# High and low halves of the columns side by side in one matmul: a hybrid decoder trunk on one core

## The chip, the core and the metric

The kernel runs on one core of a Trainium2 chip. The metric is the device time of one execution in microseconds (us), the median of three runs. Inside one profiled execution the profile also gives the span of the core's own work, from its first instruction to its last.

## What is computed

The reference is a trunk of two pre-norm residual layers over 256 tokens of width 1024, in float32. Of each layer only the mixer matters here; after it comes a dense SwiGLU (layer 0) or a top-2-of-8 expert SwiGLU (layer 1).

```python
h = rms_norm(x, norm_mix[layer])
q, f_logit, i_in, g_out, b_gate, c_gate, u, gate_a, gate_b = split_projection(h, w_in)   # 1024 columns each
f = lb + (1 - lb) * sigmoid(f_logit);  k = (1 - lb) * sigmoid(-f_logit);  q = silu(q) * scale
o = rms_norm(recurrence(q, k, i_in, log(max(f, F_MIN)))) * silu(g_out)      # 8 heads of 128
conv = causal_depthwise_conv3(b_gate * u)
merged = sigmoid(gate_a) * (o @ w_proj_hgrn) + sigmoid(gate_b) * ((c_gate * conv) @ w_proj_conv)
x = x + merged @ w_out
```

## The kernel before

**Number format.** Every float32 product is done as three matmuls in a shorter format. A weight tile `w` is split into `wh` (its high part, made by ScalarE) and `wl` (the rest, made by VectorE); the activations are split into `hh` and `hl` likewise. The product is `wh*hh + wh*hl + wl*hh`, summed in PSUM.

**A stream and its loads.** `col(s, g)` names the g-th half (512 columns) of the s-th part of `w_in`: 0 queries, 1 forget gates, 2 and 3 value and output gate, 4, 6 and 5 the convolution's b, u and c, 7 and 8 the merge gates. `mm_cols` (L125 on) computes one such half with tokens in the free dimension: it loads the weights in two pieces of 1 MB with `wload` (4 rows of 128 by 512 columns each), and for each row block `kt` of 128 and each column block `ct` of 128 it issues three matmuls with 256 moving columns (the tokens): L139 `wh` by `hh`, L141 `wh` by `hl`, L143 `wl` by `hh`. A half is 32 such triples, 96 matmuls. Its four sums stand in one PSUM tile of 4 KB a partition, tag "mm", of which there are two.

**The weights' way.** `wload` (L77 to L94) issues the load on SyncE's queue into one of four buffers (more of them late in layer 1), then ScalarE copies the high part into one of three buffers (L91, `whi`), then VectorE subtracts for the low part into one of two buffers (L93, `wlo`). For the first four loads of a mixer these two steps are cut into pieces of 512 elements.

**What follows a stream.** In `mixer` (from L515 on) a finished PSUM tile is read by one VectorE instruction of 1024 elements a partition: `by_rbc` (L258), which multiplies by the per-token factor of the norm, or for u and c a product with what is there (L596, L614). Forget gates then go through two sigmoids and nine VectorE instructions, queries through a silu and a scaling.

**What runs beside.** `scores` (prefix products of the recurrence, mostly VectorE, with small matmuls) and `readout` are generators; each `tick()` after a weight piece adds one of their steps to the program. The three-tap convolution (L604 to L607, 24 VectorE instructions) reads `bu`, the product of b and u, and writes `cv`; the product of `cv` and c is split into `ych`, `ycl` (tags hlC and hlD) for the convolution's output projection, whose first weight piece meets the first half of `cv` and the second piece the second half.

**Order.** The source is not the order of the queues. The framework that compiles it places every instruction on its engine's in-order queue as soon as its inputs are expected to be there, and in source order among those that are ready; a tile with a tag is handed over when the last reader of the tile before it on that tag is done. The column tiles `hh` and `hl` are made by `cols` (L235) on tags hlA and hlB.

## Time and profile before

| | |
|---|---|
| median of 3 runs (lowest, highest) | 1512.69 us (1511.3, 1512.91) |
| the profiled execution, its own time | 1511.85 us |
| span of the core in it | 1510.1 us |
| mean granted clock of TensorE | 0.995 of full speed |
| TensorE matmul busy | 1462.3 us (97% of the span) |
| VectorE busy | 651.4 us (43%) |
| ScalarE busy | 394.4 us (26%) |
| read from HBM | 414.40 MB |

The span holds, in order, the mixer of layer 0 (to about 311 us), the dense SwiGLU (to about 500 us), the mixer of layer 1 (to about 801 us) and the experts (to the end). The mean shares of VectorE and ScalarE say little: nearly all their work lies in the first 800 us. The profile's engines are PE (TensorE matmul), PEld (TensorE weight load), DVE (VectorE), ACT (ScalarE), POOL (GpSimd) and SP (SyncE).

### The profile page before, as it was taken

To read this page: it belongs to the slowest core of one execution; us is meant where nothing else is said; L and a number is where in the kernel's file an instruction comes from. 1 tells how busy PE (TensorE), PEld (TensorE's weight loads), DVE (VectorE), ACT (ScalarE), POOL (GpSimd) and SP (SyncE) were. 2 spreads that over 40 slices of the span, in tenths; PEclk is the share of its full clock that TensorE was granted. 3 is DMA by queue.
4 is the path that set the end of the run, shared out by engine and by line. 5 is a ranking of instruction groups with operands and counts; after the bars stand their busy time and mean duration, and the time that the engine had idled before them with its cause. 6 is when DMAs were issued, how large, how long until landed. Compare 5 with 4: busy or idle time off the path is not lost.

```text
span 1510.1 us, 39658 instructions
## 1 busy us (share of the span) xinstructions
PE 1462.3 (97%) x18130; PEld 1203.4 (80%) x18130; DVE 651.4 (43%) x875; ACT 394.4 (26%) x484; POOL 41.7 (3%) x80
## 2 busy tenths in 40 slices
PE   7999999999999999999999999899999989999994
PEld 7989999999999998999996696557977554766751
DVE  6965776665455796568764202011121102011112
ACT  6544334454344554434442000000000000000000
POOL 3000011000000000001000000000000000000000
PEclk9999999999999999999999999999999999999998
DMA  8564544556556555555746899999999999999994
GB/s 270 181 194 157 169 140 170 194 168 195 186 178 197 166 194 170 168 168 203 285 168 226 290 402 409 410 413 406 411 373 402 408 413 409 408 412 359 411 410 184
DMA packets 135364, 418.15 MB, mean 277 GB/s; under 512 B 6784, under 2 KB 8928, under 8 KB 123920
## 3 DMA queue, kind: packets, MB, share of 16 engines
q1 hardware_dynamic: 134768, 414.26, 73.9%
q8 instruction: 146, 2.39, 0.7%
q0 software_dynamic: 384, 1.21, 0.3%
q14 instruction: 34, 0.28, 0.1%
q10 hardware_dynamic: 32, 0.01, 0.0%
HBM read 414.40 MB, written 1.05 MB: 275 GB/s over the span
## 4 chain that ended last, share of the span: by engine, by line
PE 89%; DMA 9%; DVE 1%; ACT 0%; issue 0%; SPq 0%; POOL 0%; POOLq 0%; DVEq 0%; ACTq 0%
PE psb L139 12%; PE pa L982 12%; PE psb L143 12%; PE psb L141 12%; PE pb L982 11%; PE ye L972 10%; DMA wraw<-in_expert_w_dram 8%; PE psa L160 3%; PE psa L162 3%; PE psa L161 3%; PE psc L1023 2%; PE y L708 1%; PE y L709 1%; PE y L710 1%; PE pg L920 1%; PE ye L964 1%
## 5 line engine op out<-in xcount | busy, mean ns | idle before, releaser
L139 PE MATMUL psb<-hlA,whi 128*128 128x256 f32 x1376 | 393.5, 286 | 3.2 <-ACT whi L91 3.2
L143 PE MATMUL psb<-hlA,wlo 128*128 128x256 f32 x1376 | 390.4, 284 | 0.8 <-DVE wlo L93 0.8
L141 PE MATMUL psb<-hlB,whi 128*128 128x256 f32 x1376 | 390.2, 284 | 0.0
L91 ACT ACTIVATE whi<-wraw 128x2048 fp32r<-128x2048 f32 (+1 forms) x165 | 251.7, 1543 | 376.6 <-PE psb L141 234.5
L93 DVE TENSOR_TENSOR wlo<-wraw,whi 128x2048 fp32r<-128x2048 f32 (+1 forms) x165 | 297.9, 1821 | 116.3 <-issue 40.4
L139 PEld LDWEIGHTS psb<-hlA,whi 128*128 128x128 f32 x1376 | 264.3, 192 | 4.6 <-ACT whi L91 3.6
L143 PEld LDWEIGHTS psb<-hlA,wlo 128*128 128x128 f32 x1376 | 264.2, 192 | 1.5 <-DVE wlo L93 1.3
L141 PEld LDWEIGHTS psb<-hlB,whi 128*128 128x128 f32 x1376 | 264.5, 192 | 0.5
L1055 DVE TENSOR_TENSOR sae<-sae,pb 128x768 f32<-128x768 f32 (+3 forms) x24 | 19.1, 796 | 454.5 <-PE pb L982 454.5
L972 PE MATMUL ye<-wraw,the 128*32 128x256 f32 x2640 | 150.5, 379 | 1.0 <-issue 1.0
L972 PEld LDWEIGHTS ye<-wraw,the 128*32 128x32 f32 x2640 | 104.8, 110 | 39.9 <-issue 2.5
L1054 ACT ACTIVATE sae<-pa 128x768 f32<-128x768 f32 (+3 forms) x24 | 16.4, 685 | 433.1 <-PE pa L982 433.1
L982 PE MATMUL pb<-wraw,bu 128*32 128x256 f32 (+1 forms) x2112 | 109.3, 362 | 2.4 <-DMA wraw<-in_expert_w_dram 1.8
L982 PE MATMUL pa<-wraw,bu 128*32 128x256 f32 (+1 forms) x2112 | 110.0, 362 | 0.7 <-DMA wraw<-in_expert_w_dram 0.7
L982 PE MATMUL pb<-wraw,hlD 128*32 128x256 f32 (+1 forms) x1920 | 100.8, 362 | 4.0 <-DMA wraw<-in_expert_w_dram 3.9
L982 PE MATMUL pa<-wraw,hlD 128*32 128x256 f32 (+1 forms) x1920 | 102.2, 362 | 0.7 <-DMA wraw<-in_expert_w_dram 0.7
L982 PEld LDWEIGHTS pb<-wraw,bu 128*32 128x32 f32 x2112 | 74.7, 110 | 34.3 <-issue 2.8
L982 PEld LDWEIGHTS pa<-wraw,bu 128*32 128x32 f32 x2112 | 73.2, 110 | 34.0 <-issue 4.9
L982 PEld LDWEIGHTS pb<-wraw,hlD 128*32 128x32 f32 x1920 | 71.3, 110 | 30.3 <-DMA wraw<-in_expert_w_dram 5.8
L982 PEld LDWEIGHTS pa<-wraw,hlD 128*32 128x32 f32 x1920 | 72.8, 110 | 26.3 <-issue 6.4
L964 PE MATMUL ye<-wraw,the 128*64 128x512 f32 x264 | 61.8, 601 | 10.7 <-DMA wraw<-in_expert_w_dram 10.7
L964 PEld LDWEIGHTS ye<-wraw,the 128*64 128x64 f32 x264 | 17.2, 136 | 51.2 <-issue 27.1
(259 smaller groups left out, 1459.3 us busy)
## 6 DMA issues: line engine op xcount, KB each, us to landing
wraw<-in_expert_w_dram SPq DMA_DIRECT2D x216, 1024.0 KB, 17.8
wraw<-in_w_in_dram SPq DMA_DIRECT2D x72, 1024.0 KB, 5.2
wraw<-in_expert_w_dram SPq DMA_DIRECT2D x64, 768.0 KB, 15.9
wraw<-in_dense_w_dram SPq DMA_DIRECT2D x33, 1024.0 KB, 5.1
wraw<-in_w_proj_conv_dram SPq DMA_DIRECT2D x8, 1024.0 KB, 5.1
wraw<-in_w_proj_hgrn_dram SPq DMA_DIRECT2D x8, 1024.0 KB, 5.1
wraw<-in_w_out_dram SPq DMA_DIRECT2D x8, 1024.0 KB, 5.2
xt<-in_x_dram SPq DMA_DIRECT2D x2, 512.0 KB, 3.8
```

The costliest lines, as they stand in the source:

```text
L91: nc.scalar.activation(hf[:, ks], rf[:, ks], AF.Copy)
L93: nc.vector.tensor_tensor(lf[:, ks], rf[:, ks], hf[:, ks].bitcast(F32), op=ALU.subtract)
L139: nc.tensor.matmul(o, wh[:, k, cs], hh[:, kt, :], start=first, stop=False, skip_group_check=True)
L141: nc.tensor.matmul(o, wh[:, k, cs], hl[:, kt, :], start=False, stop=False, skip_group_check=True)
L143: nc.tensor.matmul(o, wl[:, k, cs], hh[:, kt, :], start=False, stop=last, skip_group_check=True)
L160: nc.tensor.matmul(o, hh[:, kt, ts], wh[:, k, :], start=kt == 0, stop=False)
L161: nc.tensor.matmul(o, hh[:, kt, ts], wl[:, k, :], start=False, stop=False)
L162: nc.tensor.matmul(o, hl[:, kt, ts], wh[:, k, :], start=False, stop=kt == KT - 1)
L964: nc.tensor.matmul(out[64 * h:64 * h + 64, 0:n], stat, w[:, h * n:h * n + n], start=start, stop=stop, skip_group_check=True)
L972: nc.tensor.matmul(out(g)[32 * lane:32 * lane + 32, 0:n], by_lane(g if lane == 3 else lane, lane), w[:, c0:c0 + n], start=start and g != 1 ...
L982: nc.tensor.matmul(ps[32 * lane:32 * lane + 32, g, 0:n // 4], xf[:, kt, 32 * g:32 * g + 32], w[:, k, lane * n // 4:(lane + 1) * n // 4], s ...
L1023: nc.tensor.matmul(ps[:, o], PT[:, w, ts], y[:, part, c], start=i == part == 0, stop=part == 1 and i in (0, 3), skip_group_check=True)
```

## The change

The column tiles are laid out anew: tag hlA now holds row blocks 0 to 3 with high and low part side by side, 256 + 256 columns for each row block, and hlB row blocks 4 to 7. A small class `Part` gives the high or the low part as before, and `both(kt)` the 512 columns together.

A new function `mm_both` computes a half of 512 columns as two chunks of 256. A chunk has one weight load of 1 MB (8 row blocks by 256 columns) and its own PSUM tile: for each of its two column blocks one bank, whose first 256 columns take `wh*hh + wl*hh` and whose other 256 take `wh*hl`. For each `kt` and `ct` there are two matmuls: `wh` by both parts (512 moving columns) and `wl` by `hh` (256). At the end of a chunk ScalarE copies the second half of the banks to SBUF and VectorE adds the first half to it.

`mm_both` takes the place of `mm_cols` in nine halves of each layer: forget gates g = 1, both halves of the queries, and both halves of the convolution's b, u and c. The factor of the norm is then applied from SBUF. Two tiles are new: `uu` (tag hlC, which `ych` takes next) and `cc` (tag bu, after the convolution has read `bu`). All else is unchanged: forget gates g = 0, the merge gates, the dense layer and the output projections stay with `mm_cols`.

```diff
--- before.py
+++ after.py
@@ -147,6 +147,35 @@
             tick()
         return ps
 
+    class Part:
+
+        def __init__(self, tiles, part):
+            self.tiles, self.part = tiles, part
+
+        def __getitem__(self, at):
+            return self.tiles[at[1] // 4][at[0], at[1] % 4, self.part, at[2]]
+
+        def both(self, kt):
+            return self.tiles[kt // 4][:, kt % 4].rearrange("p i s -> p (i s)")
+
+
+
+    def mm_both(src2d, c0, hh, out):
+        for c in range(0, out.shape[1], 2):
+            ps = psum.tile([128, 2, 2, S], F32, tag="mm", name="psb")
+            wh, wl = wload(src2d, 0, KT, c0 + c * 128, 256)
+            for kt in range(KT):
+                for ct in range(2):
+                    cs = slice(ct * 128, ct * 128 + 128)
+                    nc.tensor.matmul(ps[:, ct].rearrange("p i s -> p (i s)"), wh[:, kt, cs], hh.both(kt), start=kt == 0,
+                                     stop=False, skip_group_check=True)
+                    nc.tensor.matmul(ps[:, ct, 0], wl[:, kt, cs], hh[:, kt, :], start=False, stop=kt == KT - 1,
+                                     skip_group_check=True)
+            tick()
+            o = out[:, c:c + 2, :]
+            nc.scalar.activation(o, ps[:, :, 1, :], AF.Copy)
+            nc.vector.tensor_tensor(o, o, ps[:, :, 0, :], op=ALU.add)
+
 
     def mm_toks(src2d, c0, hh, hl, after={}):
         ps = psum.tile([128, TT, 512], F32, tag="mm", name="psa")
@@ -234,7 +263,8 @@
 
     def cols(w, half):
         if half == 0:
-            cur["x"] = [big8(tag, [128, KT, S], F32R) for tag in ("hlA", "hlB")]
+            tiles = [big8(tag, [128, KT // 2, 2, S], F32R) for tag in ("hlA", "hlB")]
+            cur["x"] = [Part(tiles, i) for i in range(2)]
         hh, hl = cur["x"]
         for j in range(half * 2, half * 2 + 2):
             ps = transposed(xt, j)
@@ -532,9 +562,12 @@
         qall = big8("qq", [128, 2, 4, S])
         fc, kk, qq = ([a[:, g] for g in range(2)] for a in (fall, kall, qall))
         for g in range(2):
-            ps = mm_cols(wi, col(1, g), 512, hh, hl, enter if g == 0 else {})
             f, k = fc[g], kk[g]
-            by_rbc(f, ps)
+            if g == 0:
+                by_rbc(f, mm_cols(wi, col(1, g), 512, hh, hl, enter))
+            else:
+                mm_both(wi, col(1, g), hh, f)
+                by_rbc(f, f)
             nc.scalar.activation(k, f, AF.Sigmoid, scale=-1.0)
             nc.scalar.activation(f, f, AF.Sigmoid)
             for i in range(4):
@@ -544,8 +577,8 @@
                 nc.vector.tensor_scalar(k[:, i, :], k[:, i, :], om[:, l, hd:hd + 1], None, op0=ALU.mult)
             nc.vector.tensor_scalar(f, f, F_MIN, None, op0=ALU.max)
         for g in range(2):
-            ps = mm_cols(wi, col(0, g), 512, hh, hl)
-            by_rbc(qq[g], ps)
+            mm_both(wi, col(0, g), hh, qq[g])
+            by_rbc(qq[g], qq[g])
             nc.scalar.activation(qq[g], qq[g], AF.Silu)
             nc.vector.tensor_scalar(qq[g], qq[g], QSCALE, None, op0=ALU.mult)
 
@@ -588,12 +621,14 @@
 
         bu = big8("bu", [128, KT, S])
         for g in range(2):
-            ps = mm_cols(wi, col(4, g), 512, hh, hl)
-            by_rbc(bu[:, g * 4:g * 4 + 4, :], ps)
+            gs = slice(g * 4, g * 4 + 4)
+            mm_both(wi, col(4, g), hh, bu[:, gs, :])
+            by_rbc(bu[:, gs, :], bu[:, gs, :])
+        uu = big8("hlC", [128, KT, S])
         for g in range(2):
-            ps = mm_cols(wi, col(6, g), 512, hh, hl)
             gs = slice(g * 4, g * 4 + 4)
-            nc.vector.tensor_tensor(bu[:, gs, :], bu[:, gs, :], ps, op=ALU.mult)
+            mm_both(wi, col(6, g), hh, uu[:, gs, :])
+            nc.vector.tensor_tensor(bu[:, gs, :], bu[:, gs, :], uu[:, gs, :], op=ALU.mult)
             by_rbc(bu[:, gs, :], bu[:, gs, :])
         flush(1)
         if l % 2 == 1:
@@ -607,11 +642,12 @@
             nc.vector.scalar_tensor_tensor(cv[:, ct, 2:S], bu[:, ct, 0:S - 2], wc(0), cv[:, ct, 2:S],
                                            op0=ALU.mult, op1=ALU.add)
         ych, ycl = (big8(tag, [128, KT, S], F32R) for tag in ("hlC", "hlD"))
+        cc = big8("bu", [128, KT, S])
         for g in range(2):
-            ps = mm_cols(wi, col(5, g), 512, hh, hl)
             gs = slice(g * 4, g * 4 + 4)
             by_rbc(cv[:, gs, :], cv[:, gs, :])
-            nc.vector.tensor_tensor(cv[:, gs, :], cv[:, gs, :], ps, op=ALU.mult)
+            mm_both(wi, col(5, g), hh, cc[:, gs, :])
+            nc.vector.tensor_tensor(cv[:, gs, :], cv[:, gs, :], cc[:, gs, :], op=ALU.mult)
             split(cv[:, gs, :], ych[:, gs, :], ycl[:, gs, :])
         if l % 2 == 1:
             more("fc")
```

## Rows read from the trace of the kernel before

**Rows 1.** The page: busy time of each engine (first row), the DMA engines' mean busy tenths in 40 slices of the span (second row), and the chain of work that ended last, by engine and by line.

```profile
PE 1462.3 (97%) x18130; PEld 1203.4 (80%) x18130; DVE 651.4 (43%) x875; ACT 394.4 (26%) x484; POOL 41.7 (3%) x80
...
DMA  8564544556556555555746899999999999999994
...
PE 89%; DMA 9%; DVE 1%; ACT 0%; issue 0%; SPq 0%; POOL 0%; POOLq 0%; DVEq 0%; ACTq 0%
PE psb L139 12%; PE pa L982 12%; PE psb L143 12%; PE psb L141 12%; PE pb L982 11%; PE ye L972 10%; DMA wraw<-in_expert_w_dram 8%; PE psa L160 3%; PE psa L162 3%; PE psa L161 3%; PE psc L1023 2%; PE y L708 1%; PE y L709 1%; PE y L710 1%; PE pg L920 1%; PE ye L964 1%
```

**Rows 2.** Busy time by stretch. Columns: the stretch and its length in us, then for PE, PEld, DVE, ACT and POOL the busy us and in brackets the number of instructions, then the granted clock, the share of the DMA engines and GB/s. The stretches are those of layer 0: forget gates g = 1 and queries; the convolution's b; u; c.

```profile
27.00:61.40 34.40, 34.40 (x289) 34.40 (x288) 33.62 (x43) 19.37 (x13) 0.00 (x0) 1.00 0.53 176
...
159.50:186.00 26.50, 26.50 (x419) 25.80 (x405) 20.88 (x31) 9.82 (x10) 0.41 (x2) 1.00 0.50 169
186.00:214.00 28.00, 28.00 (x250) 27.46 (x248) 20.72 (x29) 10.73 (x20) 1.95 (x1) 1.00 0.39 126
214.00:240.80 26.80, 26.80 (x228) 26.80 (x228) 22.81 (x39) 11.33 (x29) 7.85 (x5) 1.00 0.44 145
```

**Rows 3.** Timeline of PE over the queries' first half (layer 0): start in us, length, engine, line, operation. Its first triple and its last matmul.

```profile
38.44 0.28 PE L139 MATMUL psb<-hlA,whi 128*128 128x256 f32 x1
38.56 0.28 PE L141 MATMUL psb<-hlB,whi 128*128 128x256 f32 x1
38.68 0.28 PE L143 MATMUL psb<-hlA,wlo 128*128 128x256 f32 x1
...
49.84 0.28 PE L143 MATMUL psb<-hlA,wlo 128*128 128x256 f32 x1
```

**Rows 4.** Timeline of PE in a value stream (512 moving columns): one triple, from one L160 to the next; the two matmuls between are left out.

```profile
70.38 0.39 PE L160 MATMUL psa<-whi,hlA 128*128 128x512 f32 x1
...
71.06 0.39 PE L160 MATMUL psa<-whi,hlA 128*128 128x512 f32 x1
```

**Rows 5.** Timeline of PE where 256 columns give way to 512 (288 us) and 512 to 256 (311 us).

```profile
288.45 0.28 PE L143 MATMUL psb<-hlA,wlo 128*128 128x256 f32 x1
288.57 0.40 PE L160 MATMUL psa<-whi,hlC 128*128 128x512 f32 x1
...
311.04 0.39 PE L162 MATMUL psa<-whi,hlD 128*128 128x512 f32 x1
311.26 0.28 PE L139 MATMUL psb<-hlA,whi 128*128 128x256 f32 x1
```

**Rows 6.** Groups of instructions by line with shapes kept apart: line, engine, operation, tiles, shapes, count | busy us, mean ns of one | idle time of the engine before them and its releasers. Two of DVE (an addition that reads PSUM; a product out of SBUF), then three of ACT and DVE (a copy out of PSUM; the two steps on the weights).

```profile
L644 DVE TENSOR_TENSOR xt<-xt,psa 128x512 f32<-128x512 f32 x8 | 5.2, 684 | 3.5 <-PE psa L673 2.3 <-PE psa L162 1.1
...
L258 DVE TENSOR_TENSOR bu<-bu,rbc 128x1024 f32<-128x1024 f32 x4 | 4.9, 1220 | 0.0
...
L413 ACT ACTIVATE st<-psx 128x512 f32<-128x512 f32 x4 | 2.3, 579 | 0.0
...
L91 ACT ACTIVATE whi<-wraw 128x2048 fp32r<-128x2048 f32 x117 | 224.3, 1917 | 357.4 <-PE psb L141 232.9 <-issue 91.5 <-PE psa L162 19.1
L93 DVE TENSOR_TENSOR wlo<-wraw,whi 128x2048 fp32r<-128x2048 f32 x117 | 267.5, 2286 | 107.0 <-issue 38.1 <-PE psa L161 22.9 <-PE psb L143 21.9
```

**Rows 7.** DMA over a stretch of the dense layer (446 to 460 us) in which weight pieces of 256 columns are loaded: packets by size, and the issues with size and median time to landing; the third row is the page's for the pieces of 512 columns.

```profile
DMA packets 2279, 2.52 MB, mean 180 GB/s; under 512 B 32, under 2 KB 2080, under 8 KB 2278
...
wraw<-in_dense_w_dram SPq DMA_DIRECT2D x3, 1024.0 KB, 5.4
...
wraw<-in_w_in_dram SPq DMA_DIRECT2D x72, 1024.0 KB, 5.2
```

**Rows 8.** Who waited for whom: the waiter, what it waited for: us in total, times, longest us.

```profile
ACT whi L91 <- PE psb L141: 234.5, 68, 4.7
```

**Rows 9.** Timeline of DVE beside the queries' first half: a reciprocal of the scores, the factor on forget gates g = 1, and the low part of the first weight piece of the queries' second half.

```profile
38.33 2.54 DVE L344 RECIPROCAL bu<-fc 128x384 f32<-128x384 f32 x1
40.79 1.15 DVE L258 TENSOR_TENSOR fc<-psb,rbc 128x1024 f32<-128x1024 f32 x1
...
47.01 2.27 DVE L93 TENSOR_TENSOR wlo<-wraw,whi 128x2048 fp32r<-128x2048 f32 x1
```

**Rows 10.** Timeline of DVE beside the convolution's c: the product of b and u (second half), the last instructions of the convolution, and the low part of the first weight piece of c, g = 1.

```profile
214.47 1.21 DVE L596 TENSOR_TENSOR bu<-bu,psb 128x1024 f32<-128x1024 f32 x1
...
223.67 0.87 DVE L607 SCALAR_TENSOR_TENSOR fc<-bu,pcol,fc 128x254 f32<-128x254 f32 x2
...
225.31 2.28 DVE L93 TENSOR_TENSOR wlo<-wraw,whi 128x2048 fp32r<-128x2048 f32 x1
```

**Rows 11.** Timeline of PE: last matmul of c, g = 0, first of c, g = 1, last of c, g = 1, first of the convolution's output projection.

```profile
227.34 0.28 PE L143 MATMUL psb<-hlA,wlo 128*128 128x256 f32 x1
...
229.17 0.36 PE L139 MATMUL psb<-hlA,whi 128*128 128x256 f32 x1
...
240.64 0.28 PE L143 MATMUL psb<-hlA,wlo 128*128 128x256 f32 x1
240.76 0.28 PE L139 MATMUL psb<-hlC,whi 128*128 128x256 f32 x1
```

**Rows 12.** Timeline of ACT and then of DVE after the end of c, g = 1: the next high part, the high part of the product, and its low part.

```profile
240.89 1.92 ACT L91 ACTIVATE whi<-wraw 128x2048 fp32r<-128x2048 f32 x1 [3.84 <-PE psb L141]
242.71 1.04 ACT L55 ACTIVATE hlC<-fc 128x1024 fp32r<-128x1024 f32 x1
...
244.30 1.22 DVE L56 TENSOR_TENSOR hlD<-fc,hlC 128x1024 fp32r<-128x1024 f32 x1
```

## The prediction

> **What bounds the kernel now.** I read the chain of waits first: PE holds 89% of it, the DMA engines 9%, VectorE 1% [rows 1]. The DMA share is the experts' weights: only in the last third of the slices are the DMA engines at 9 tenths and over [rows 1]. Then the busy times of the stretches that the change touches: PE is busy through all of them, at a granted clock of 1.00, the 2.4 GHz level; the DMA engines are at 0.39 to 0.53 [rows 2]. So in the mixer the end is set by the time between matmul starts. Beside it VectorE is the engine to watch: 33.6 of 34.4 us in the forget gates and queries, 21 to 23 of some 27 us in the convolution's streams [rows 2]. Third, the timelines of PE, DVE and ACT at the places where a stream ends, for how early each input of PE was ready. Whatever the two mixers gain or lose comes through to the end: the dense layer and the experts wait for them, and the expert weights' loads are released by the weight buffers that the mixer frees, which move with PE.
>
> **What the change takes away.** A half of 512 columns is 96 matmuls. From the first to the last of the queries' first half there are 95 steps in 49.84 - 38.44 = 11.40 us, so 120 ns from start to start with 256 moving columns [rows 3]. With 512 moving columns three steps take 71.06 - 70.38 = 0.68 us, 226.7 ns each [rows 4]. At 2.4 GHz the columns alone are 106.7 and 213.3 ns: both carry some 13.3 ns that do not grow with the columns. Two matmuls of 256 by the same weights are 240.0 ns, one of 512 is 226.7. A triple falls from 360.0 to 346.7 ns. The new order alternates the two sizes, and the trace has each passage once: 256 to 512 in 0.12 us, 512 to 256 in 0.22 us [rows 5], as if each ran among its like. I count nothing for it. 32 triples a half, nine halves a layer, two layers: 576 x 13.3 ns = **7.7 us less** on PE. The bounds of this term: the two passages of rows 5 add up to 0.34 us to the rounding of the rows, 0.35 at most, which would leave 10 ns a triple and 5.8 us; more than 7.7 no row shows.
>
> The Trainium skill (TensorE: Matmul & The Clock Gate, Back-to-back issue gap) puts the warm gap of a matmul by itself at its columns over 2.4 GHz plus 2.5 ns. By that a merged pair would save 2.5 ns and the change 1.4 us. The trace shows 13.3 ns in both sizes, so the measurement decides.
>
> **What it adds off PE.** Each of 36 chunks ends with a ScalarE copy of 512 elements out of PSUM, 0.58 us, and a VectorE addition that reads PSUM, 0.68 us [rows 6]: 21 us of ScalarE and 24.6 us of VectorE in all. The factor of the norm, 1.22 us, reads SBUF and not PSUM and costs the same [rows 6]. The weight loads stay as many and as large. Their rows shrink from 2 KB to 1 KB; the dense layer's last pieces have that shape already and land in 5.4 us against 5.2 [rows 7], four buffers ahead, with the DMA engines half idle. Nothing.
>
> The copy does not run at once. A new high part starts on ScalarE in the moment in which a chunk's matmuls free its buffer (68 such waits, 234.5 us [rows 8]). In a chunk the last matmul by `wh` stands one step ahead of the last by `wl`, so the 1.92 us high part [rows 6] is ready first and the copy stands behind it on the in-order queue. The sum of a chunk is then in SBUF some 1.92 + 0.58 + 0.68 + 0.2 (hand-overs, an estimate) = 3.4 us after its last matmul, 1.5 if the copy goes first. A chunk lasts 16 x 346.7 = 5.55 us, and PE needs that PSUM tile again one chunk later: 2.1 us to spare. So the shorter life of the PSUM tiles costs nothing where VectorE is free.
>
> **What is late next.** Three places have less room, each once a layer.
>
> *Queries.* The low part of the second half's first piece stands behind all the forget gates' work. It ends at 47.01 + 2.27 = 49.28 us, and PE needs it at 49.96 + 0.24 = 50.20 [rows 3, 9] (the half's last start plus one step, then two more): 0.9 us to spare. Two additions come ahead of it (0.68 each) and PE arrives 2 x 0.43 us sooner: 1.3 us short if all else keeps its place. But VectorE was full there with work that PE does not wait for yet, like the 2.54 us reciprocal at 38.33 us [rows 9]; some of it will move back. Between 0 and 1.3, I take 0.3.
>
> *The convolution's c.* `cc` takes over the buffer of `bu`, so no chunk of c leaves PSUM before the convolution has read its last `bu`: 223.67 + 0.87 = 224.5 us, and the low part after it ends at 227.6, while PE needs it at 229.17 + 0.24 = 229.4 [rows 10, 11]: 1.8 us to spare. From the end of u's first half to there VectorE gets four additions more (2.7 us) and PE comes 0.87 us sooner; that is 1.8 us short. Against it, the readout's products and a factor of the norm may move back, 2.3 us by their neighbours' rows. Between 0 and 3 (the sum and the delayed copy), I take 0.6.
>
> *The start of the output projection.* Its second piece, 48 steps of 120 ns after 240.76 us, at 246.5, needs the second half of the product of `cv` and c; that was ready at 244.30 + 1.22 = 245.5 [rows 11, 12], 1.0 us to spare. Before, the product (1.22 us) ran beside the high part of the weights (240.89 to 242.81 [rows 12]). Now it stands behind copy and addition, which stand behind that high part: 0.13 + 1.92 + 0.58 + 0.68 + 1.22 + 1.04 + 1.22 = 6.8 us after the last matmul's end, with hand-overs some 7, against 5.9 needed. 1.0 us short; 0 if the copy goes first. Between 0 and 2, I take 1.0.
>
> In b and u themselves VectorE keeps some 5 us of idle time in 26.5 [rows 2] against 2.7 us of additions in each stretch: nothing, at most 0.5.
>
> **The sum.** 7.7 less, 2 x (0.3 + 0.6 + 1.0) = 3.8 more: 3.9 us less. The profiled execution (1511.85 us, of which 1510.1 are the span) would come to 1508.0; the median of the runs stands 0.84 us above that execution, so **1508.8 us**.
>
> **The rivals.**
> - *The gain in full.* The copies go ahead of the high parts, and VectorE's deferrable work moves back at all three places. For it: that work is there [rows 9]. Against it: the high parts started at the first moment 68 times [rows 8]. 1512.7 - 7.7 = 1505.0 us.
> - *The gain is eaten.* All three places fall short by their full sums, 1.3 + 1.8 + 1.0 = 4.1 us a layer, 8.2 in all: 1513.2; with one of them half covered, 1511 to 1512. For it: VectorE at 98% in the queries [rows 2].
> - *Slower: c's sums wait for the convolution.* One mechanism: the handing over of `bu`'s buffer to `cc`. PE can do two chunks of c (11.1 us and the readout's matmuls between, some 2.7: 229.17 - 227.34 - 0.12 = 1.7 of them [rows 11], the rest within the half) before it needs the first PSUM tile back; from then on each us that the convolution ends later is a us of PE. If the product of b and u starts 3.4 us after u's last matmul, and two low parts (2.29 each) are placed ahead of the convolution's last instructions, its end is 3.4 + 4.6 = 8 us later than the 11.2 us after u's end of now (213.3 to 224.5), 19.2, and the copy and addition bring it to 20.5 against 13.8. 6.7 us a layer, 13.4 in all, less 7.7: 1518.4 us. It decides for slower from 3.9 us a layer on. Against it: the convolution stands ahead of those low parts in the source, and what is ready goes in source order.
> - *The merge saves nothing.* The 13.3 ns come back with the alternation of sizes, as a 360 ns triple: 0 less, 3.8 more, 1516.5 us. Rows 4 and 5 speak against it. The skill's 2.5 ns, if they held for this pair, would give 1512.7 - 1.4 + 3.8 = 1515.1 us.
>
> **How the numbers follow.** Forecast (1506.5 to 1509.7) 0.33; gain in full 0.20; eaten 0.28; merge saves nothing 0.06; slower 0.13. A measurement of this kernel tells about 0.2%, 3.0 us, from no change. Faster by more than that: forecast and full gain, 0.53. Within: the eaten gain, 0.28. Slower by more: the last two, 0.19. The range takes in the full gain and half a us below it, and above all of the eaten case with 2 us for the bounds of its terms: 1504.5 to 1515.5, with the last two rivals left out. The forecast's own range is 1506.5 to 1509.7.
>
> **What the profile after would show.** 512-column matmuls of `whi` by hlA or hlB, 576 of them, with starts 226.7 ns apart from the next, and triples of 347 ns; if the triple is 360 ns, the first term is wrong. ScalarE's copies 2 us after a chunk's last matmul, behind a high part; if they come at once, the third place has no wait. PE waiting for `wlo` in the queries, for the PSUM tile or `wlo` at c's g = 1, for hlD in the first projection: 0.3, 0.6 and 1.0 us, the same in both layers. A wait of PE for ScalarE or VectorE at every chunk, some us each, would mean that the sums come back later than one chunk, and would prove the whole account of the PSUM tiles wrong.

## The result, and the profile after

| | median of its runs | profiled execution | span | ratio to before |
|---|---|---|---|---|
| before | 1512.19 us (4 runs) | 1511.85 us | 1510.1 us | |
| after | 1522.54 us (4 runs) | 1522.33 us | 1520.6 us | 1.0056 [1.0038, 1.0073] |

The medians differ by 10.35 us. (The ratio is an estimate of its own with a 95% interval, not the quotient of these two medians.) The forecast was 1508.8 us, and the range ended at 1515.5. The question is where more than the gain went.

First, the merge. This is the timeline of PE early in forget gates g = 1, which begin at 30.02 us: the fourth pair of matmuls and the start of the fifth (start in us, length, engine, line, operation).

```profile
31.08 0.40 PE L170 MATMUL psb<-hlA,whi 128*128 128x512 f32 x1
31.31 0.28 PE L172 MATMUL psb<-hlA,wlo 128*128 128x256 f32 x1
31.43 0.40 PE L170 MATMUL psb<-hlA,whi 128*128 128x512 f32 x1
```

From start to start there are 0.23 and 0.12 us, so what was a triple takes 0.35 us; the forecast was 346.7 ns. The two sizes in alternation don't eat the gain, but it isn't whole everywhere: this half took 11.31 us, 353 ns a triple, and the queries' second half in layer 1 took 11.09 us, 346.6 ns.

Second, what PE waited for. Apart from the wait for the very first high part (4.1 us, before 3.2), three rows of its waits belong to the streams of the mixers and are new or longer (waiter, what it waited for: us in total, times, longest us; both layers together):

```profile
PE psb L172 <- DVE wlo L93: 4.2, 4, 1.7
...
PE psb L143 <- DVE wlo L93: 3.1, 3, 1.3
PE psb L139 <- ACT hlC L55: 0.4, 2, 0.2
```

The first two are waits for the weights' low part, which VectorE makes; before, those of L143 came to 0.8 us in all. The third is the convolution's projection, which waits for the high part of its input. None is for a PSUM tile.

Third, where. The start of every stream of weights can be read from the timeline of PE, and the difference of two starts is a stream's length. Sorted by parts, the span grew by 10.5 us so:

| part | change, us |
|---|---|
| up to the end of the first stream (forget gates g = 0, not merged) | +3.1 |
| forget gates g = 1 and queries, layers 0 and 1 | -0.5, -0.9 |
| b and u | -1.5, -1.5 |
| c and the first half of the convolution's projection | +5.5, +5.3 |
| the other streams of the mixers and the dense layer | -0.2 |
| experts and the stretch ahead of them | +1.1 |

So the merge gave 4.4 us in the streams ahead of c, and c with the projection's start took 10.8. The first and the last part hold no merged stream. At the start 1.0 us is the later begin of the first stream (13.28 against 12.30 us), and 2.1 us its pace. The windows after (the stretch and its length, busy us and instructions of PE, PEld, DVE, ACT and POOL, granted clock, DMA share, GB/s):

```profile
12.00:17.00 5.00, 3.72 (x15) 3.26 (x15) 3.66 (x9) 4.40 (x11) 1.74 (x4) 0.52 1.08 358
17.00:27.00 10.00, 9.54 (x60) 9.42 (x60) 7.54 (x19) 6.89 (x14) 0.53 (x1) 0.73 0.99 297
...
214.70:246.30 31.60, 29.21 (x178) 24.87 (x178) 27.45 (x42) 15.07 (x36) 5.88 (x5) 1.00 0.43 143
```

From 17 to 27 us the granted clock was 0.73 after and 1.00 before. The timeline of PE shows it too: the matmuls of the first stream start 0.21 us apart until 22.5 us, before until 16.9, and then 0.12. PE left the 1.2 GHz level 5.6 us later in this execution; ahead of that stream it had stood idle, 4.1 us of it for the first high part (3.2 before). The experiments show whether that is a price of the change. The third row is c's stretch: PE is busy 29.2 of 31.6 us at the full clock, where before it was busy all the time [rows 2]. It is c that has to be explained.

There, in layer 0, PE reads as follows (idle time before an instruction, and who ended it, in brackets):

```profile
230.36 0.50 PE L170 MATMUL psb<-hlA,whi 128*128 128x512 f32 x1
230.70 1.75 PE L253 MATMUL pst<-ident,tokA 128*128 128x128 f32 x9
232.38 0.50 PE L170 MATMUL psb<-hlA,whi 128*128 128x512 f32 x1
234.58 0.39 PE L172 MATMUL psb<-hlA,wlo 128*128 128x256 f32 x1 [1.70 <-DVE wlo L93]
...
240.02 0.71 PE L253 MATMUL pst<-ident,tokA 128*128 128x128 f32 x5
241.14 0.39 PE L172 MATMUL psb<-hlA,wlo 128*128 128x256 f32 x1 [0.42 <-DVE wlo L93]
...
254.97 0.39 PE L143 MATMUL psb<-hlC,wlo 128*128 128x256 f32 x1 [1.35 <-DVE wlo L93]
```

The first matmul by the low part of c, g = 1, comes 4.2 us after the first by the high part; before it was two steps, 0.24 us. The marked wait is only part of the loss: 14 of the readout's transposes (L253), which stood behind the projection's first half, now lie in this gap (9) and in the next (5). VectorE's timeline shows why the low part came late:

```profile
217.41 2.29 DVE L93 TENSOR_TENSOR wlo<-wraw,whi 128x2048 fp32r<-128x2048 f32 x1
...
219.69 0.68 DVE L177 TENSOR_TENSOR hlC<-hlC,psb 128x512 f32<-128x512 f32 x1
...
221.17 1.22 DVE L631 TENSOR_TENSOR bu<-bu,hlC 128x1024 f32<-128x1024 f32 x1
...
227.38 0.86 DVE L642 SCALAR_TENSOR_TENSOR fc<-bu,pcol,fc 128x254 f32<-128x254 f32 x2
...
228.49 1.22 DVE L288 TENSOR_TENSOR fc<-fc,rbc 128x1024 f32<-128x1024 f32 x1
229.63 0.68 DVE L177 TENSOR_TENSOR bu<-bu,psb 128x512 f32<-128x512 f32 x1
...
231.65 0.68 DVE L177 TENSOR_TENSOR bu<-bu,psb 128x512 f32<-128x512 f32 x1
232.24 2.28 DVE L93 TENSOR_TENSOR wlo<-wraw,whi 128x2048 fp32r<-128x2048 f32 x1
```

Before, the second product of b and u started at 214.47 us, the convolution ended at 224.5 and the low part was ready at 227.6 [rows 10], 14.3 us after u's end (by which I mean the start of what PE runs behind u's last matmul, 213.3 us). Now the product starts at 221.17, because it waits for the sums of u. Counted from u's end, now at 214.3, that is 6.9 us, and before it was 1.2. ScalarE shows the first part of that delay:

```profile
214.44 1.91 ACT L91 ACTIVATE whi<-wraw 128x2048 fp32r<-128x2048 f32 x1 [3.01 <-issue]
216.26 0.26 ACT L466 ACTIVATE tokA<-pso 128x128 f32<-128x128 f32 x1
...
217.26 0.62 ACT L176 ACTIVATE hlC<-psb 128x512 f32<-128x512 f32 x1
```

The last copy of u, at 217.26, stood behind a high part and the readout's squares (four such pairs of L466 in 216.26 to 217.26), and its addition, at 219.69, behind the low part of 217.41 on VectorE. The convolution follows and ends at 228.2 us, 13.9 after u's end; before it was 11.3. So of the 5.7 us by which the product starts later, only 2.7 are left at the convolution's end, mainly because the low part that ran behind the product before (at 215.60 us) now runs ahead of it. The rest comes behind the convolution, where a factor, two additions of c and products of the readout stand ahead of the low part. It is ready at 234.5 us, 20.2 after u's end, 5.9 more than before. The factor on `cv` is there by the change itself, as the diff shows and the description of the change doesn't say: `by_rbc(cv)` stood behind each half of c in the source and now stands ahead of it.

### The profile page after: what moved, and what is told of

Its sections match the earlier page's. It is cut to its first block, busy times and chain, and to the rows that moved or that the text cites. A ratio compares the mean times of both kernels' runs of the same rounds, so it can differ in the third digit from the quotient of the medians.

```text
span 1520.6 us, 38574 instructions
## 1 busy us (share of the span) xinstructions
PE 1462.4 (96%) x17554; PEld 1157.5 (76%) x17554; DVE 672.2 (44%) x911; ACT 411.1 (27%) x520; POOL 36.3 (2%) x80
## 4 chain that ended last, share of the span: by engine, by line
PE 82%; DMA 10%; DVE 5%; POOL 1%; issue 1%; ACT 1%; SPq 0%; POOLq 0%; DVEq 0%; ACTq 0%
PE pa L1018 12%; PE pb L1018 10%; PE ye L1008 10%; DMA wraw<-in_expert_w_dram 9%; PE psb L143 7%; PE psb L139 7%; PE psb L141 7%; PE psb L170 7%; PE psb L172 3%; PE psa L189 3%; PE psa L191 3%; PE psa L190 3%; PE psc L1059 2%; DVE wlo L93 2%; PE y L745 1%; PE y L744 1%
## 5 line engine op out<-in xcount | busy, mean ns | idle before, releaser
L139 PE MATMUL psb<-hlA,whi 128*128 128x256 f32 x464 | 133.6, 288 | 4.1 <-ACT whi L91 4.1
L143 PE MATMUL psb<-hlA,wlo 128*128 128x256 f32 x464 | 133.2, 287 | 0.5 <-DVE wlo L93 0.5
L1008 PEld LDWEIGHTS ye<-wraw,the 128*32 128x32 f32 x2640 | 97.6, 110 | 46.5 <-issue 2.3
L141 PE MATMUL psb<-hlB,whi 128*128 128x256 f32 x464 | 131.5, 283 | 0.0
L170 PE MATMUL psb<-hlA,whi 128*128 128x512 f32 x288 | 105.3, 404 | 0.0
L170 PE MATMUL psb<-hlB,whi 128*128 128x512 f32 x288 | 102.6, 396 | 0.0
L141 PE MATMUL psb<-hlA,whi 128*128 128x256 f32 x336 | 96.6, 288 | 0.0
L139 PE MATMUL psb<-hlB,whi 128*128 128x256 f32 x336 | 96.0, 286 | 0.0
L143 PE MATMUL psb<-hlB,wlo 128*128 128x256 f32 x336 | 95.3, 283 | 0.0
L139 PEld LDWEIGHTS psb<-hlA,whi 128*128 128x128 f32 x464 | 90.7, 195 | 4.8 <-ACT whi L91 4.3
L1018 PEld LDWEIGHTS pb<-wraw,hlD 128*32 128x32 f32 x1920 | 67.4, 110 | 32.6 <-DMA wraw<-in_expert_w_dram 4.7
```

The costliest lines, as they stand in the source:

```text
L139: nc.tensor.matmul(o, wh[:, k, cs], hh[:, kt, :], start=first, stop=False, skip_group_check=True)
L141: nc.tensor.matmul(o, wh[:, k, cs], hl[:, kt, :], start=False, stop=False, skip_group_check=True)
L143: nc.tensor.matmul(o, wl[:, k, cs], hh[:, kt, :], start=False, stop=last, skip_group_check=True)
L170: nc.tensor.matmul(ps[:, ct].rearrange("p i s -> p (i s)"), wh[:, kt, cs], hh.both(kt), start=kt == 0, stop=False, skip_group_check=True)
L1008: nc.tensor.matmul(out(g)[32 * lane:32 * lane + 32, 0:n], by_lane(g if lane == 3 else lane, lane), w[:, c0:c0 + n], start=start and g != 1 ...
L1018: nc.tensor.matmul(ps[32 * lane:32 * lane + 32, g, 0:n // 4], xf[:, kt, 32 * g:32 * g + 32], w[:, k, lane * n // 4:(lane + 1) * n // 4], s ...
```

## Experiments

Three theories could explain that chain. *Buffer*: the sums of c can't leave PSUM before `bu` is free (my rival for slower). *Late copies* (A): the copy behind the high part starts everything late. *VectorE* (B and C): either its additions are simply too much work there (B), or the place of the low part in its in-order queue is the cause, behind a convolution that PE does not wait for (C). The lengths that the verdicts rest on, in us, layer 1 of the profiled executions, from the first matmul of a stream to the first of the next (S is the four halves of the gates that the change leaves as they were); the last column has layer 0 beside it, where c's column behaves otherwise in some runs:

| | f g=1, queries | S | b, u | c and first projection half | the same, layer 0 |
|---|---|---|---|---|---|
| before | 34.56 | 51.01 | 54.49 | 39.86 | 39.86 |
| after | 33.66 | 51.01 | 53.00 | 45.20 | 45.34 |
| e1, layout alone | 34.56 | 51.01 | 54.48 | 39.86 | 39.86 |
| e2, all but c | 33.67 | 51.01 | 53.00 | 40.23 | 42.32 |
| e3, c alone | 34.56 | 51.01 | 54.47 | 41.63 | 41.68 |
| e4, cc in its own buffer | 33.67 | 51.01 | 52.83 | 48.24 | 46.21 |
| e5, copy first | 36.13 | 51.01 | 53.31 | 44.74 | 45.58 |
| e6, no addition | 35.74 | 51.01 | 53.01 | 42.06 | 42.45 |
| e7, third low buffer | 33.98 | 51.01 | 53.02 | 45.21 | 45.34 |
| e8, gates too, not c | 33.99 | 49.28 | 53.00 | 40.67 | 43.79 |
| e9, late convolution | 33.69 | 51.01 | 52.83 | 41.54 | 41.58 |
| e10, e8 with it | 33.67 | 49.30 | 52.83 | 40.23 | 40.27 |
| e11, all merged with it | 33.69 | 49.30 | 52.83 | 41.53 | 41.58 |

With the full saving of 0.85 us, c's column would be 39.0. Two merged halves give at most 0.85, three 1.28 and four 1.71.

**e1, the layout without the merge.** Every `mm_both` goes back to `mm_cols`; the parts of the columns stay side by side.

```diff
-            mm_both(wi, col(0, g), hh, qq[g])
-            by_rbc(qq[g], qq[g])
+            by_rbc(qq[g], mm_cols(wi, col(0, g), 512, hh, hl))
```

> The new layout of the columns alone, no merged matmul: every stream with mm_cols. Theory (the loss lies in the convolution's c; the 2.7 us that the changed kernel loses before its second stream and the 1.5 us in the experts are the scatter of single executions): the same as before, 1512 us, within 2. Rival (the layout itself costs at the mixer's start): 1515 to 1516.5.

1514.87 us against 1514.01 of the kernel before on the same chip, ratio 1.0002 [0.9991, 1.0013]. (The table above has 3.1 us where the expectation has 2.7; it is 2.7 if counted from PE's first instruction. Likewise 1.1 stands there for its 1.5.) The streams from the second to the last projection's first half are as before, to 0.1 us in all. Its first stream took 16.80 us, though, as in the kernel after (16.73), against 14.62 before, and the second half of the last projection with the way to the experts 26.4 against 24.0 (before and after). So both outer parts of the decomposition vary without the merge. e6, with the same layout, had 14.59 us in the first stream; so the layout alone doesn't set its length. A price of the layout within the interval, up to some 2 us, is not excluded.

**e2, all but c; e3, c alone.**

```diff
-        cc = big8("bu", [128, KT, S])
...
+            ps = mm_cols(wi, col(5, g), 512, hh, hl)
...
-            mm_both(wi, col(5, g), hh, cc[:, gs, :])
-            nc.vector.tensor_tensor(cv[:, gs, :], cv[:, gs, :], cc[:, gs, :], op=ALU.mult)
+            nc.vector.tensor_tensor(cv[:, gs, :], cv[:, gs, :], ps, op=ALU.mult)
```

> The changed kernel with c back on mm_cols, the other seven halves of a layer merged. Theory: the 5.3 us a layer that the traces show between the start of c and the first output projection go away, the savings of the other streams (2.0 us in layer 0, 2.2 in layer 1) stay: 1512.2 - 4.2 = 1508, up to 1511 if the mixer's start costs. Rival (additions in VectorE's queue cost wherever they stand): half of the loss stays, 1514 to 1518.

In e3 queries, forget gates, b and u go back to `mm_cols` as in e1, and c stays as in the changed kernel:

```diff
-            mm_both(wi, col(4, g), hh, bu[:, gs, :])
-            by_rbc(bu[:, gs, :], bu[:, gs, :])
+            by_rbc(bu[:, gs, :], mm_cols(wi, col(4, g), 512, hh, hl))
```

> Only c merged, all other streams with mm_cols. Theory: c alone carries the loss, 1512.2 + 2 x 5.3 = 1523, a little less because u's sums come back sooner: 1519 to 1523. Rival (the loss needs the late product of b and u, which comes from u's own copy and addition): 1512 to 1515.

e2: 1512.96 us, ratio 0.9992 [0.9982, 1.0001]. e3: 1519.92 us, ratio 1.0039 [1.0027, 1.0050]. c carries most of the loss, but e2's gain falls short: its theory had 1508 to 1511, which would be a ratio of at most 0.9992, and in layer 0 c's column is still 2.5 us longer than before (42.32 against 39.86) with c not merged at all, from u's late sums alone. In layer 1 that is 0.4. In e3 c's streams by themselves account for less than e3's whole ratio: they grow by 1.8 us in either layer, 3.6 in all, 0.24%; its profiled execution also had 27.6 us instead of 24.0 ahead of the experts and 16.2 instead of 14.6 in the first stream, which e1 showed to vary. In c's column merging c alone falls 2.6 us short of the full saving (41.63 to 39.0), and with u merged as well 6.2 (45.20 to 39.0). So the two together cost more than the sum of either alone, c's 2.6 and u's 0.4 in layer 1.

**e4, `cc` in its own buffer.** The queries' buffer is free by then.

```diff
-            more("qq", "kk")
+            more("kk")
...
-        cc = big8("bu", [128, KT, S])
+        cc = big8("qq", [128, KT, S])
...
-            more("fc")
+            more("fc", "qq")
```

> The changed kernel with the tile cc on the queries' buffer, which is free by then, so that c's sums need not wait until the convolution has read bu; in layer 1 that buffer joins the ring of weight buffers later. Theory (the handing over of bu's buffer holds PSUM and PE): c loses 1 to 2 us a layer and not 5.3, 1514 to 1516. Rival (VectorE is simply full there, so the low parts are late whatever the buffer): 1520 to 1523.

1523.49 us, ratio 1.0065 [1.0048, 1.0083]: no gain. Its VectorE at the same place:

```profile
226.51 0.88 DVE L642 SCALAR_TENSOR_TENSOR fc<-bu,pcol,fc 128x254 f32<-128x254 f32 x2
...
227.63 0.68 DVE L177 TENSOR_TENSOR qq<-qq,psb 128x512 f32<-128x512 f32 x1
...
231.62 2.28 DVE L93 TENSOR_TENSOR wlo<-wraw,whi 128x2048 fp32r<-128x2048 f32 x1
```

The first addition of c comes sooner (227.63 against 229.63; 1.2 us of that if counted from the start of c), but still behind the convolution's last instruction, and the low part stands behind the second. The buffer theory falls, and with it the mechanism of my rival. (Other instructions shift with the buffer: against before, c's column grew by 6.4 us in layer 0 and by 8.4 in layer 1.)

**e5, the copy first.** The high part that takes over a chunk's buffer is put behind that chunk's copy.

```diff
-            nc.scalar.activation(o, ps[:, :, 1, :], AF.Copy)
+            copied = nc.scalar.activation(o, ps[:, :, 1, :], AF.Copy)
+            if not ring["order"]:
+                ring["order"].append((None, None))
+            ring["order"].append((copied, None))
```

> The changed kernel with ScalarE's copy of a chunk's sums placed ahead of the high part that becomes free in the same moment, so that the sums come back 1.9 us sooner. Theory A (the sums come back late: the copy's place behind the high part delays the product of b and u, the convolution and all behind it): c loses 2 to 3 us a layer and not 6, the time falls by 6 to 8 us against the changed kernel, to 1515. Theory B (VectorE has too much to do between u's end and the projection, whatever the copy does): it stays within 2 us of the changed kernel, 0.6% over before.

1530.29 us, ratio 1.0093 [1.0076, 1.0110], which neither theory had: c's column gains only 0.5 us and the queries lose 2.5. Waits of PE, and VectorE behind u:

```profile
PE psb L172 <- DVE wlo L93: 9.5, 7, 2.1
...
PE psa L193 <- DVE wlo L93: 3.2, 2, 1.6
```

```profile
223.02 1.22 DVE L634 TENSOR_TENSOR bu<-bu,hlC 128x1024 f32<-128x1024 f32 x1
...
224.23 2.29 DVE L93 TENSOR_TENSOR wlo<-wraw,whi 128x2048 fp32r<-128x2048 f32 x1
...
232.24 0.87 DVE L645 SCALAR_TENSOR_TENSOR fc<-bu,pcol,fc 128x254 f32<-128x254 f32 x2
```

A high part put later makes a low part later. The product of b and u does start sooner, 4.2 us after u's end (218.9) and not 6.9, but a low part now follows it, and the convolution ends 14.2 us after u's end and not 13.9. So the early copy by itself buys nothing there. The edit is not a clean trial of A, though: c's copy waits for the convolution, and a high part of c now waits behind it. e9 tells more on A.

**e6, no addition**, which tests B.

```diff
-            nc.vector.tensor_tensor(o, o, ps[:, :, 0, :], op=ALU.add)
```

> The changed kernel without VectorE's 72 additions: the sums are the copied half alone, so the part of the product that the first half of each bank holds is left out of the output. Theory B (VectorE's work): 72 x 0.68 us less of VectorE's queue, c loses at most 2 us a layer, 1510 to 1514. Theory A (the late copy): only 0.7 us of each delay of 3.4 goes, c still loses 4 to 5 us a layer, 1518 to 1520.

The expectation counts 72 additions; the kernel after has 36, one a chunk, so 24.5 us of VectorE's time go. 1526.28 us, ratio 1.0078 [1.0059, 1.0097]. The router sees other values, so only the mixers are read, and they lie between the two: c's column falls from 45.20 to 42.06, so 3.1 of the 6.2 us go and 3.1 stay, where B had at most 2 and A 4 to 5. VectorE then PE:

```profile
227.41 1.22 DVE L287 TENSOR_TENSOR fc<-fc,rbc 128x1024 f32<-128x1024 f32 x1
...
229.52 1.13 DVE L473 SCALAR_TENSOR_TENSOR tokA<-pso,orr,tokB 128x128 f32<-128x128 f32 x4 [0.90 <-POOL orr L469]
230.57 4.48 DVE L93 TENSOR_TENSOR wlo<-wraw,whi 128x2048 fp32r<-128x2048 f32 x2
```

```profile
232.90 0.39 PE L172 MATMUL psb<-hlA,wlo 128*128 128x256 f32 x1 [2.64 <-DVE wlo L93]
```

Without one addition the low part still stands behind the factor and the readout's products, even through 0.90 us in which VectorE waits for GpSimd's `orr` and does nothing. So the order counts, and not the work alone. (The queries became 2.1 us longer; why was not followed up.)

**e7, a third buffer for low parts during c**, in case the low part waits for a buffer.

```diff
+        ring["lo"] = deque([None, None, "qq"])
...
-            more("qq", "kk")
+            more("kk")
...
+        ring["lo"] = deque([None])
...
-            more("fc")
+            more("fc", "qq")
```

> The changed kernel with a third buffer for the low parts while c is loaded (the queries' buffer, free by then), so that a low part may be made a chunk earlier. If what holds PE is only the low part's place in VectorE's queue behind the convolution, c loses 2 us a layer, 1514 to 1516. If VectorE has no idle time left there (theory B), or if the copies' lateness sets it (theory A), it stays within 2 us of the changed kernel.

1525.30 us, ratio 1.0056 [1.0035, 1.0078]; c's column 45.21, and the low part starts where it did:

```profile
232.29 2.29 DVE L93 TENSOR_TENSOR wlo<-wraw,whi 128x2048 fp32r<-128x2048 f32 x1
```

So it is no buffer. By its expectation this result speaks for A or B; but the buffer did not change the low part's place in the queue, so it says nothing against the place as the cause.

**e8, the other gates merged too, and c not.**

```diff
-                ps = mm_cols(wi, col(s, g), 512, hh, hl)
...
-                by_rbc(sg[s][:, gs, :], ps)
+                mm_both(wi, col(s, g), hh, sg[s][:, gs, :])
+                by_rbc(sg[s][:, gs, :], sg[s][:, gs, :])
```

> c on mm_cols as before, and the four halves of the merge gates merged as well, where VectorE is busy 29 of 51 us: eleven merged halves a layer. If a merged half saves its 0.43 us wherever VectorE has room: 22 x 0.43 = 9.4 less than before, less 1 to 3 for what c and the queries give back, a ratio of 0.995 to 0.996. If the copies and additions cost wherever they stand: 0.999 to 1.002.

1511.62 us, ratio 0.9979 [0.9960, 0.9998]. The four halves fall by 1.73 us, 0.43 each: the full saving, where VectorE has room. The total saves less than the theory's 0.995 to 0.996, and its interval reaches into the rival's range; only the lengths of the streams tell the two apart. In layer 0 c's column, not merged here, gave back 3.9 us (43.79 against 39.86), as in e2.

**e9, the second half of the convolution late**, which tests C. It is the kernel after with `cc` as in e4, and the convolution's last four column tiles and their factor written behind the matmuls of c, g = 1. VectorE does the same work; only its order changes.

```diff
+        conv(range(4))
...
-            by_rbc(cv[:, gs, :], cv[:, gs, :])
+            if g == 0:
+                by_rbc(cv[:, gs, :], cv[:, gs, :])
             mm_both(wi, col(5, g), hh, cc[:, gs, :])
+            if g == 1:
+                conv(range(4, KT))
+                by_rbc(cv[:, gs, :], cv[:, gs, :])
```

> The changed kernel with cc on the queries' buffer and the second half of the convolution (12 VectorE instructions) written behind the stream of c, g = 1, so that the low parts of c's weights come first in VectorE's queue. All nine halves stay merged and no work is taken away. Theory C (what holds PE is that the low part for c's third chunk stands in VectorE's in-order queue behind the product, the convolution and the additions, which end later than before): c and the first projection lose at most 2 us a layer and not 6, a ratio of 0.997 to 1.000. Theory B (VectorE has more to do there than time): the loss only moves to the projection, 1.003 to 1.006.

1513.51 us, ratio 0.9998 [0.9989, 1.0007], against 1.0065 [1.0048, 1.0083] of e4, which has the same buffers. VectorE now, and PE's wait in the projection:

```profile
219.20 1.22 DVE L631 TENSOR_TENSOR bu<-bu,hlC 128x1024 f32<-128x1024 f32 x1
...
220.60 1.22 DVE L288 TENSOR_TENSOR bu<-bu,rbc 128x1024 f32<-128x1024 f32 x1
...
222.25 2.28 DVE L93 TENSOR_TENSOR wlo<-wraw,whi 128x2048 fp32r<-128x2048 f32 x1
...
226.77 0.61 DVE L640 TENSOR_SCALAR fc<-bu,pcol 128x256 f32<-128x256 f32 x2
...
227.69 2.29 DVE L93 TENSOR_TENSOR wlo<-wraw,whi 128x2048 fp32r<-128x2048 f32 x1
```

```profile
241.08 0.39 PE L143 MATMUL psb<-hlC,wlo 128*128 128x256 f32 x1 [0.95 <-DVE wlo L93]
```

The low part is made at 222.25 us, ahead of the convolution, and ahead of its first half too, which still stands before c's stream in the source: the framework's order moved with the edit. The second half of c takes 11.18 us (16.21 after, 11.59 before, layer 1), the full saving, with no wait. The sums of u are as late as in the kernel after (the product starts 6.9 us after u's end, 212.3, in both), and VectorE does the same work; so neither A nor B is what held PE in c, and theory C is shown for c. (The edit also puts the second factor on `cv` behind the stream again; what each of the two brings was not told apart.) What is left, 2.5 us a layer in c's column, lies mostly in the projection's first half (15.12 against 13.19), where PE waits for low parts beside the rest of the convolution; whether work or order sets that was not tried.

**e10 and e11, what is best.** e10 is e8 with the late convolution (eleven merged halves a layer, c not); e11 is e9 with the gates of e8 (thirteen). Their edits are those above.

> The merge gates merged, c on mm_cols, and the second half of the convolution written behind c's second stream. Theory C: the 2 to 3 us that layer 0 still gives back in c go too, a ratio of 0.994 to 0.997. Theory B: as with the gates alone, 0.998.

> All thirteen halves of a layer but forget gates g = 0 merged, with the late second half of the convolution and cc on the queries' buffer. Theory C: 26 x 0.43 = 11.1 us less, 2 to 4 given back, a ratio of 0.994 to 0.997. Theory B: 1.000 to 1.003.

e10: 1508.39 us against 1513.43, ratio 0.9963 [0.9949, 0.9977]. e11: 1510.63 us, 0.9979 [0.9969, 0.9988]. e10 came out as theory C had it, e11 between the two ranges. In layer 0 c's column goes from e8's 43.79 to 40.27 us by the late convolution alone. In e10 the waits for low parts have gone from the mixers but for one row:

```profile
PE psb L143 <- DVE wlo L93: 0.4, 1, 0.4
```

e10 is faster than both kernels: the merge pays where the sums have time. With c merged as well (e11) c's column is 1.3 us longer.

## Why the prediction failed, by its steps

- **The term of the merge was right in kind, and a little too large.** Its 13.3 ns a triple are there in the second half of the queries in layer 1 (11.52 to 11.09 us) and in the halves of S in e8 (0.43 us each); b and u give 0.37 a half. Forget gates g = 1 give 0.21, so 7 ns a triple, less than the prediction's lower bound of 10. The seven merged halves ahead of c gave 4.4 us in the two layers together, where the term has 6.0. PE's chain was read rightly, and the DMA term: 1 MB pieces of the mixers land in 5.1 us after, also where all pieces have the halved rows.
- **The account of the PSUM tiles was right** as far as b, u and the gates go: no wait for a PSUM tile there, and 1.5 us saved of 1.7 in b and u ("nothing, at most 0.5").
- **Queries.** Taken 0.3 us a layer, for a low part that comes late. Forget gates and queries gave 0.5 and 0.9 us of 1.28, so 0.8 and 0.4 are missing, near the 0.3 in layer 1 but by luck: no wait for a low part stands there. What is missing is in the pace, up to 353 ns a triple instead of 346.7. What sets that pace stays open; it differs between runs (33.72 us in layer 0 of e9, 34.04 after, with nothing changed in these streams).
- **The convolution's c is the step that failed.** Taken 0.6, bounds 0 to 3 a layer. In layer 1, c's two halves took 31.41 us instead of 25.82 with the full saving; 1.5 of that are the moved transposes (14 at some 0.11 us), so c lost some 4.1 us. Two things in it were wrong. First, the sum counted four additions (2.7 us) and PE's gain, but not that the *start* of the product of b and u moves: 6.9 us after u's end and not 1.2. The prediction had worked out 3.4 us for the return of a sum, and used it only in the rival. It was more: 6.1 us from u's end (214.3) to the end of its last addition (219.69 + 0.68), since the readout's squares and a low part stood ahead as well. Second, I let the readout's products and a factor of the norm "move back" by 2.3 us. They did not: the convolution, the factor and c's first two additions stood ahead of the low part in VectorE's queue, the factor by the change's own order of the source. The low part had 1.8 us to spare before, and was 4.0 us late after (PE's first matmul by it at 234.58 us, due at 230.6).
- **The start of the output projection.** Taken 1.0, bounds 0 to 2. Measured 0.6 in the length of its first half, and 1.5 of transposes that it no longer holds: 2.1 us a layer. The wait is for the low part and for `hlC` and not for hlD, which I had named.
- **The rival for slower** had the place, the source (sums late, low parts ahead of the convolution) and nearly the size (6.7 us a layer; measured 6.2 to 6.4 in that place), but not the mechanism: it was to be the buffer of `bu`, and e4 took that away without a gain. So its size was near by luck. Its counter-argument, that the convolution stands ahead of the low parts in the source, names the cause of the loss: that order makes PE wait for work that PE doesn't need yet.
- **The sum.** By lengths of streams: -4.4 + 10.8 = 6.4 us, 0.42%, which lies in the measured interval [1.0038, 1.0073]; the forecast had 7.7 less and 3.8 more. The remaining 4.1 us between the two profiled executions stand in the start and at the experts, and differ as much without the merge (4.7 in e1).

## What to carry to other kernels

A shorter stream on the bounding engine pays only if the engine that gets the extra work does not also make the bounding engine's next input: look for the last step of that input (here the low part of the weights), and list what stands ahead of it in its in-order queue and when the last of that can start. Count by how much the start of that work moves, and not only the length of the new instructions; then check in the timeline how much of the delay is left at the end, since other work moves ahead meanwhile. Where the queue is the limit, write work that the bounding engine doesn't wait for behind the input that it does wait for; that alone turned 1.0065 into 0.9998 here. With c not merged it gave the fastest kernel, 0.9963; without it the same eleven halves had 0.9979, and the two intervals overlap.

## What the runs showed of the hardware that was not expected

PE's time beyond the columns is per matmul and about the same for both sizes: alternating 512 and 256 columns started 0.23 and 0.12 us apart, and where the saving was whole a saved matmul gave back 0.43 us / 32 = 13.4 ns. In other halves, without a marked wait, it gave back about half of that (11.31 us for 11.52).

VectorE holds its order even when its next instruction waits: in e6 a low part that PE needed next, its high part long made (220.57 + 1.91 us), stood behind products whose factor GpSimd had not yet made, and VectorE did nothing for 0.90 us. The Trainium skill (PSUM — Partial Sum Buffer, Engine vs sequencer instructions) describes the queues of ScalarE and VectorE as strictly first in, first out; this row agrees.

The moment at which PE's pace goes from 0.21 to 0.12 us a step at the start differs between profiled executions: 16.9 us before, 17.8 in e6, and 20.4 to 22.9 in the other eleven. It is worth some 2 us of the first stream (14.6 us in the first two, 16.2 to 16.9 in the others), and no edit separates the two groups, though only one execution of the old layout was profiled; what decides it stays open. The granted clock doesn't always show it. In e1 PE's timeline and the window around it read

```profile
18.23 0.41 PE L143 MATMUL psb<-hlA,wlo 128*128 128x256 f32 x1
18.45 0.41 PE L139 MATMUL psb<-hlA,whi 128*128 128x256 f32 x1
```

```profile
17.00:21.00 4.00, 4.00 (x19) 4.00 (x20) 3.88 (x9) 3.74 (x8) 0.00 (x0) 1.00 0.96 284
```

so steps of 0.22 us stand beside a clock of 1.00: in the first 25 us the pace of the matmuls is the better witness.
